# Loading half of b's first slice ahead of a in a fused matmul, GELU, matmul kernel

## Chip, cores and metric

One core of one Trainium2 chip. The metric is the device time of one execution in microseconds (us).

## The reference

```python
def reference(a, b, c):            # a 1024x1024, b 1024x2048, c 2048x1024, all float32
    h = np.matmul(a, b)
    h = 0.5 * h * (1 + np.tanh(np.sqrt(2 / np.pi) * (h + 0.044715 * h ** 3)))
    return np.matmul(h, c)
```

## The kernel before

PE is the engine of the matrix products, DVE and ACT are the vector and the scalar engine, and SP issues the loads. The kernel loads the first four row blocks of a (a0 to a3, 512 KB each) and then the left halves of b's eight row blocks ("slices" b0 to b7, 128 rows of 4 KB, 512 KB each) through one queue. Each block of a is cast to bf16 (DVE one half, ACT the other), transposed on PE and copied into `aT`. Products of zeros, at the start and between the transposes, keep PE busy so that its clock rises; those between are called fillers below. The first real products (k=0) need all four blocks of a and b0; those of k=1 need b1, and so on. What follows k=7 (the rest of the two matrix products) is not touched by the change.

```python
    def load_b0(k, parts):
        st = b0stage.tile([128, W0], F32, name="b0_st")
        w = W0 // parts                                   # W0 = 1024 columns
        for i in range(parts):
            nc.sync.dma_start(out=st[:, ts(i, w)], in_=bv[:, k, ts(i, w)])
        b_st[k] = st

    for mt in R:                                          # a0 .. a3
        load_a0(mt, 1)
    for k in range(KT):                                   # b0 .. b7
        load_b0(k, 1)
    # ... cut
    warm_up(8)                                            # 8 products of zeros
    # ... cut: cast_a0, turn0 (transposes), copy0, cast_b0
    for mt in range(3):
        cast_a0(mt, 0)
        cast_a0(mt, 1)
        pt = [turn0(mt, 0), turn0(mt, 1)]
        if mt == 2:
            cast_a0(3, 0)
        copy0(mt, 0, pt[0])
        copy0(mt, 1, pt[1])
        warm_up((3, 6, 2)[mt])
    copy0(3, 0, turn0(3, 0))                              # with b0's casts inside
    warm_up(2)
    # ... cut
    for t in R:
        mm0(t, (0,))                                      # first k=0 products
    copy0(3, 1, turn0(3, 1))
    for t in (4, 7, 6, 5):
        mm0(t, (0,))
```

Of the kernel before, what the change touches and what calls it, by code (L numbers as in the profile page):

```python
# [9 lines left out]
F32 = mybir.dt.float32  # L10
# [9 lines left out]
def kernel(ctx, tc, a, b, c, out):  # L20
    nc = tc.nc
# [3 lines left out]
    KT = K // 128  # L25
# [4 lines left out]
    W0 = N // 2  # L30
# [5 lines left out]
    bv = b.rearrange("(kt p) n -> p kt n", p=128)  # L36
# [7 lines left out]
    b0stage = ctx.enter_context(tc.tile_pool(name="b0stage", bufs=6))  # L44
# [19 lines left out]
    a_st, b_st = {}, {}  # L64

    def load_a0(mt, parts):
        st = astage.tile([128, K], F32, name="a_st")
        w = K // parts
        for i in range(parts):
            nc.sync.dma_start(out=st[:, ts(i, w)], in_=av[:, mt, ts(i, w)])  # L70
        a_st[mt] = st

    def load_b0(k, parts):
        st = b0stage.tile([128, W0], F32, name="b0_st")
        w = W0 // parts
        for i in range(parts):
            nc.sync.dma_start(out=st[:, ts(i, w)], in_=bv[:, k, ts(i, w)])  # L77
        b_st[k] = st

    gate = consts.tile([128, 1], F32, name="gate")  # L80
    for mt in R:
        load_a0(mt, 1)
    for k in range(KT):
        load_b0(k, 1)

    nc.gpsimd.tensor_copy(gate, b_st[4][:, 0:1])
    g = consts.tile([128, 1], F32, name="g")
# [5 lines left out]
    def warm_up(n):  # L93
        for _ in range(n):
            nc.tensor.matmul(ps[3], warm[:, 0:128], warm, start=True, stop=True)  # L95
# [4 lines left out]
    def cast_a0(mt, g):  # L100
        if g == 0:
            ab.append(abf.tile([128, K], BF16, name="ab1"))
            nc.vector.tensor_copy(ab[mt][:, 0:512], a_st[mt][:, 0:512])
        else:
            nc.scalar.activation(ab[mt][:, 512:K], a_st[mt][:, 512:K], AF.Copy)

    def turn0(mt, g):
        if mt == 2:
            pt = side[g]
        elif (mt, g) == (3, 1):  # L110
            pt = ps[5][:, :].bitcast(BF16).rearrange("p (k m) -> p k m", k=8)
        else:
            pt = tpool.tile([128, 8, 128], BF16, name="pt", tag="pt")
        for k in range(4):
            nc.tensor.transpose(pt[:, k, :], ab[mt][:, ts(4 * g + k, 128)], ident)
        return pt

    def copy0(mt, g, pt):
        dst = aT[0][:, ts(g, 4), ts(mt, 128)]
        if g == 0 and mt == 3:  # L120
            nc.vector.tensor_copy(dst[:, 0, :], pt[:, 0, :])
            cast_b0(0, (0,))
            nc.vector.tensor_copy(dst[:, 1:4, :], pt[:, 1:4, :])
            cast_b0(0, (1,))
        elif g == 0 or mt == 3:
            nc.vector.tensor_copy(dst, pt[:, 0:4, :])
        else:
            nc.scalar.activation(dst, pt[:, 0:4, :], AF.Copy)

    HW = W0 // 2  # L130

    def cast_b0(k, parts=(0, 1)):
        v = {0: ((128, 384), (768, W0)), 1: ((0, 128), (128, HW))}.get(k, ((0, HW),))
        a = {0: ((0, 128), (384, 768))}.get(k, ((HW, W0),))
        for i in parts:
            if i < len(a):
                nc.scalar.activation(b_lo[:, k, slice(*a[i])], b_st[k][:, slice(*a[i])], AF.Copy)  # L137
            if i < len(v):
                nc.vector.tensor_copy(b_lo[:, k, slice(*v[i])], b_st[k][:, slice(*v[i])])  # L139

    for mt in range(3):
        cast_a0(mt, 0)
        cast_a0(mt, 1)
# [6 lines that stand above are left out]
    copy0(3, 0, turn0(3, 0))  # L150
    warm_up(2)
    ps += [ppool.tile([128, H], F32, name="ps", tag="ps") for _ in range(2)]
# [12 lines left out]
    for t in (4, 7, 6, 5):  # L165
        mm0(t, (0,))
    cast_b0(1)
    for k in range(1, KT):
        if k + 1 < KT:
# [15 lines left out]
    for j in R:  # L185
        st = abf.tile([128, K], BF16, name="ab1")
# [288 lines left out]
```

## Time and profile before

| kernel before | |
|---|---|
| device time, median of 6 runs | 120.81 us (120.11 to 121.13) |
| span of the profile | 119.0 us |
| PE busy | 96% |
| a0 lands, a3 lands | about 4.0, about 8.8 us |
| first product of k=0, of k=1 | 10.43, 12.73 us |

The prediction shows most lines of this profile. Five more are needed to compare with later: DVE's first cast of a0 and PE's six fillers from the timeline (start, length, then the instruction; in brackets the idle time before it and what ended it), the DMA view of a0's issue (its last number is the time from issue to landing), and two stretches of the windows view. In the timeline, a line has start, length, then the instruction; in brackets the idle time before it and what ended it. In the windows view, the fields after the stretch are its length, the busy time of PE, PEld, DVE, ACT and POOL, each with its count, then the granted clock, the DMA share and GB/s.

```profile
4.01 0.43 DVE L103 CAST ab<-a_st 128x512 bf16<-128x512 f32 x1 [2.88 <-DMA a_st<-in_a_dram]
...
7.41 1.46 PE L95 MATMUL ps<-warm 128*128 128x512 bf16 x6
...
a_st<-in_a_dram SPq DMA_DIRECT2D x1, 512.0 KB, 3.2
...
2.00:4.00 2.00, 2.00 (x6) 0.76 (x5) 0.00 (x0) 0.22 (x2) 0.00 (x0) 1.00 0.97 369
9.00:11.00 2.00, 1.97 (x17) 1.01 (x15) 1.44 (x6) 1.53 (x4) 0.00 (x0) 1.00 0.87 242
```

Loads run at 369 GB/s while a0 comes in and at 242 GB/s in a slow stretch from 9 to 11 us, where b0 ends and b1 begins. The six fillers take 0.24 us each (1.46 / 6), so the array is at full clock by 7.4 us.

### The profile page before, as it was taken

How to read it: one execution, taken by the hardware profiler on the slowest of the kernel's cores; microseconds unless marked ns; L12 is line 12 of the kernel's file. 1: busy time of each engine (PE TensorE's matmuls, PEld its weight loads, DVE VectorE, ACT ScalarE, POOL GpSimd, SP SyncE). 2: the span in 40 equal slices, each digit the busy share in tenths (PEclk: the TensorE clock that was granted, in tenths of full speed). 3: DMA queues.
4: the chain of work that ended last, by engine and by line, in shares of the span. 5: the costliest groups of instructions: out<-in, count | busy, mean ns of one | idle time of the engine just before them, and what ended most of it. 6: DMA issues, size and time to landing. Idle time of an engine off the chain costs nothing.

```text
span 119.0 us, 1605 instructions
## 1 busy us (share of the span) xinstructions
PE 114.7 (96%) x589; PEld 76.6 (64%) x589; DVE 82.4 (69%) x115; ACT 45.7 (38%) x77; POOL 26.6 (22%) x39
## 2 busy tenths in 40 slices
PE   5999999999999999999999999999999999999990
PEld 2555344479744445888888447888888888886460
DVE  0335433057999927999999999995789992724450
ACT  4366455788423474406269999421000000000000
POOL 2000049752310000086305229100006500000000
PEclk9999999999999999999999999999999999999999
DMA  3999999999999999959999999999997999944434
GB/s 135 379 376 286 419 419 225 169 331 391 232 211 202 206 207 358 361 130 241 258 233 205 191 194 200 182 204 147 149 162 164 248 267 348 348 168 161 175 118 148
DMA packets 13543, 28.41 MB, mean 239 GB/s; under 512 B 992, under 2 KB 5472, under 8 KB 13536
## 3 DMA queue, kind: packets, MB, share of 16 engines
q0 software_dynamic: 9216, 17.83, 72.9%
q1 hardware_dynamic: 4176, 10.42, 23.4%
q8 instruction: 4, 0.07, 0.2%
q10 hardware_dynamic: 144, 0.07, 0.2%
q14 instruction: 3, 0.02, 0.1%
HBM read 20.97 MB, written 4.19 MB: 211 GB/s over the span
## 4 chain that ended last, share of the span: by engine, by line
PE 87%; DMA 8%; SPq 2%; DVE 0%; issue 0%
PE ps L273 63%; PE ps L157 8%; DMA b_st<-in_b_dram 8%; PE ps L211 7%; PE ps L204 4%; PE pt L157 3%; PE ps L197 2%; SPq L70 1%; SPq L77 0%; DVE ot L444 0%; DVE b_lo L139 0%
## 5 line engine op out<-in xcount | busy, mean ns | idle before, releaser
L273 PE MATMUL ps<-t,s 128*128 128x512 f32 x64 | 14.9, 392 | 0.0
L273 PE MATMUL ps<-c,h 128*128 128x512 bf16 (+2 forms) x80 | 14.2, 337 | 0.0
L273 PEld LDWEIGHTS ps<-t,s 128*128 128x128 f32 x64 | 12.0, 188 | 2.6
L281 DVE TENSOR_TENSOR ot<-ps,v 128x512 f32<-128x512 f32 x16 | 10.4, 680 | 3.2 <-PE ps L273 3.2
L273 PE MATMUL ps<-t,h 128*128 128x512 f32 x48 | 11.7, 389 | 0.0
L157 PE MATMUL ps<-aT,b_lo 128*128 128x512 bf16 x48 | 11.6, 380 | 0.1
L175 ACT ACTIVATE h<-ot 128x512 bf16<-128x512 f32 (+1 forms) x16 | 9.4, 623 | 5.9 <-DVE ot L281 5.9
L273 PEld LDWEIGHTS <-h 128*128 128x128 bf16 x80 | 7.1, 98 | 7.0 <-issue 0.5
L175 ACT ACTIVATE h<-ps 128x512 bf16<-128x512 f32 (+2 forms) x17 | 8.3, 526 | 8.4 <-PE ps L211 5.9
L389 DVE TENSOR_TENSOR ot<-ps,p 128x512 f32<-128x512 f32 x11 | 7.5, 687 | 5.3 <-PE ps L273 3.1
L157 PEld LDWEIGHTS <-b_lo 128*128 128x128 bf16 x64 | 6.0, 98 | 7.8 <-DVE b_lo L139 1.0
L273 PEld LDWEIGHTS ps<-t,h 128*128 128x128 f32 x48 | 9.0, 188 | 1.9
L95 PE MATMUL ps<-warm 128*128 128x512 bf16 x21 | 7.7, 511 | 1.2 <-DVE warm L50 1.2
L211 PE MATMUL ps<-aT,b_lo 128*128 128x512 bf16 x40 | 8.8, 379 | 0.0
L291 POOL DMA_DIRECT2D c<-in_c_dram x8 | 6.3, 833 | 6.2 <-DMA b<-in_b_dram 3.9
L273 PE MATMUL ps<-as,bt 128*128 128x512 f32 x32 | 7.6, 396 | 0.0
L273 PE MATMUL ps<-as,b 128*128 128x512 f32 x32 | 7.4, 389 | 0.0
L273 PE MATMUL ps<-c,s 128*128 128x512 f32 x32 | 7.4, 389 | 0.0
L139 DVE CAST b_lo<-b_st 128x512 bf16<-128x512 f32 (+3 forms) x10 | 3.6, 371 | 5.2 <-DMA b_st<-in_b_dram 5.2
L137 ACT ACTIVATE b_lo<-b_st 128x512 bf16<-128x512 f32 (+2 forms) x9 | 5.1, 581 | 5.1 <-DMA b_st<-in_b_dram 5.0
L273 PE MATMUL ps<-aT,bx 128*128 128x512 bf16 x32 | 7.1, 379 | 0.0
L422 POOL DMA_DIRECT2D t<-c x4 | 3.5, 1042 | 15.4 <-PE ps L273 14.3
(73 smaller groups left out, 172.9 us busy)
## 6 DMA issues: line engine op xcount, KB each, us to landing
b_st<-in_b_dram SPq DMA_DIRECT2D x8, 512.0 KB, 9.6
out_dram<-ot SPq DMA_DIRECT2D x15, 256.0 KB, 2.1
c<-in_c_dram POOLq DMA_DIRECT2D x6, 512.0 KB, 17.5
t<-c POOLq DMA_DIRECT2D x6, 512.0 KB, 6.5
a_st<-in_a_dram SPq DMA_DIRECT2D x4, 512.0 KB, 4.9
b<-in_b_dram POOLq DMA_DIRECT2D x2, 1024.0 KB, 11.0
c<-in_c_dram POOLq DMA_DIRECT2D x2, 1024.0 KB, 20.3
t<-t POOLq DMA_DIRECT2D x4, 512.0 KB, 8.6
```

The lines of the kernel that those rows point to most:

```text
L95: nc.tensor.matmul(ps[3], warm[:, 0:128], warm, start=True, stop=True)
L137: nc.scalar.activation(b_lo[:, k, slice(*a[i])], b_st[k][:, slice(*a[i])], AF.Copy)
L139: nc.vector.tensor_copy(b_lo[:, k, slice(*v[i])], b_st[k][:, slice(*v[i])])
L157: nc.tensor.matmul(ps[t], b_lo[:, k, ts(t, 128)], aT[0][:, k, :], start=(k == 0), stop=(k == KT - 1))
L175: nc.scalar.activation(dst, src, AF.Gelu_apprx_tanh)
L204: nc.tensor.matmul(p, b_lo[:, k, ts(t, 128)], aT[1][:, k, ts(q, 256)], start=(k == 0), stop=(k == KT - 1))
L211: nc.tensor.matmul(p, b_lo[:, k, ts(t, 128)], aT[h][:, k, :], start=(k == 0), stop=(k == KT - 1))
L273: nc.tensor.matmul(p, lhs(t)[:, ts(j, 128)], rhs(t)[:, q], start=(t == 0), stop=(t == n - 1))
L281: tt(ot, p, u, op=ADD)
L291: nc.gpsimd.dma_start(out=dst[:, t:t + 4, :], in_=cv[:, r * NH + t:r * NH + t + 4, ts(q, H)])
L389: tt(ot, p, u, op=ADD)
L422: nc.gpsimd.dma_start(out=t2[i], in_=c21[:, P2[i], :], accum_op=ADD)
```

## The change

The intent is to have half of b0 cast while ACT has nothing to do, so that the first products need not wait for b0 and its casts. The first 512 columns of b0 are loaded ahead of a0, the other 512 behind a3; `load_b0` now takes the columns to load.

```diff
+    HW = W0 // 2
+    load_b0(0, slice(0, HW))
     for mt in R:
         load_a0(mt, 1)
-    for k in range(KT):
-        load_b0(k, 1)
+    load_b0(0, slice(HW, W0))
+    for k in range(1, KT):
+        load_b0(k)
 ... in copy0, between the copies of a3's first half:
             nc.vector.tensor_copy(dst[:, 0, :], pt[:, 0, :])
-            cast_b0(0, (0,))
+            cast_b0(0, (1,))
             nc.vector.tensor_copy(dst[:, 1:4, :], pt[:, 1:4, :])
-            cast_b0(0, (1,))
 ... in cast_b0, the columns of k=0:
-        v = {0: ((128, 384), (768, W0)), ...   # DVE
-        a = {0: ((0, 128), (384, 768))} ...    # ACT
+        v = {0: ((0, 0), (768, W0)), ...
+        a = {0: ((0, HW), (HW, 768))} ...
 ... ahead of the loop over a's blocks:
+    cast_b0(0, (0,))
```

More of the change, by code (lines that the diff above doesn't have):

```diff
@@ L71, in load_a0, with load_b0 @@
         a_st[mt] = st
-    def load_b0(k, parts):
-        st = b0stage.tile([128, W0], F32, name="b0_st")
-        w = W0 // parts
-        for i in range(parts):
-            nc.sync.dma_start(out=st[:, ts(i, w)], in_=bv[:, k, ts(i, w)])
-        b_st[k] = st
+    def load_b0(k, c=slice(0, W0)):
+        if k not in b_st:
+            b_st[k] = b0stage.tile([128, W0], F32, name="b0_st")
+        nc.sync.dma_start(out=b_st[k][:, c], in_=bv[:, k, c])
+    HW = W0 // 2
     gate = consts.tile([128, 1], F32, name="gate")
+    load_b0(0, slice(0, HW))
     for mt in R:
         load_a0(mt, 1)
-    for k in range(KT):
-        load_b0(k, 1)
+    load_b0(0, slice(HW, W0))
+    for k in range(1, KT):
+        load_b0(k)
     nc.gpsimd.tensor_copy(gate, b_st[4][:, 0:1])
@@ L128, in copy0 @@
             nc.scalar.activation(dst, pt[:, 0:4, :], AF.Copy)
-    HW = W0 // 2
     def cast_b0(k, parts=(0, 1)):
-        v = {0: ((128, 384), (768, W0)), 1: ((0, 128), (128, HW))}.get(k, ((0, HW),))
-        a = {0: ((0, 128), (384, 768))}.get(k, ((HW, W0),))
+        v = {0: ((0, 0), (768, W0)), 1: ((0, 128), (128, HW))}.get(k, ((0, HW),))
+        a = {0: ((0, HW), (HW, 768))}.get(k, ((HW, W0),))
         for i in parts:
@@ L137, in cast_b0 @@
                 nc.scalar.activation(b_lo[:, k, slice(*a[i])], b_st[k][:, slice(*a[i])], AF.Copy)
-            if i < len(v):
+            if i < len(v) and v[i][1]:
                 nc.vector.tensor_copy(b_lo[:, k, slice(*v[i])], b_st[k][:, slice(*v[i])])
+    cast_b0(0, (0,))
     for mt in range(3):
```

## The prediction

> **What bounds the kernel now.** I began with the page's busy shares: PE is busy for 96% of a 119.0 us span at full granted clock, so only PE's idle time and its start can be won. Next came the chain of work that ended last, by line and then in order of time. The kernel before, page and chain in order of time:
>
> ```profile
> PE 87%; DMA 8%; SPq 2%; DVE 0%; issue 0%
> ...
> 3.20 9.22 DMA b_st<-in_b_dram
> 12.43 0.02 issue
> 12.45 0.24 DVE b_lo L139
> 12.69 0.05 issue
> 12.73 1.52 PE ps L157 x6
> 14.26 0.21 PE pt L157
> ```
>
> The columns of the lines with a number first are start, length, what. From 12.73 us to the end the chain is almost nothing but PE. What starts that run is the landing of b's second slice (k=1) at 12.43, cast by DVE for 0.24. The DMA issued at 3.20 is the sixth of the queue: a0 to a3, b0, b1, 512 KB each. Everything earlier (a's casts and transposes, the k=0 products) matters only if it ends after that landing. Would it? The timeline of the first 16 us, PE and its weight loads, answers:
>
> ```profile
> 9.58 0.39 PE L115 MATMUL pt<-ident,ab 128*128 128x128 bf16 x4
> 9.80 0.59 PE L95 MATMUL ps<-warm 128*128 128x512 bf16 x2
> 10.43 1.04 PE L157 MATMUL ps<-aT,b_lo 128*128 128x512 bf16 x4
> 11.37 0.40 PE L115 MATMUL ps<-ident,ab 128*128 128x128 bf16 x4
> 11.60 0.38 PE L157 MATMUL ps<-aT,b_lo 128*128 128x512 bf16 x1
> 11.81 0.59 PE L157 MATMUL pt<-aT,b_lo 128*128 128x512 bf16 x2
> 12.28 1.98 PE L157 MATMUL ps<-aT,b_lo 128*128 128x512 bf16 x7
> ...
> 10.43 0.55 PEld L157 LDWEIGHTS <-b_lo 128*128 128x128 bf16 x4 [0.53 <-ACT b_lo L137]
> ...
> 12.73 0.10 PEld L157 LDWEIGHTS <-b_lo 128*128 128x128 bf16 x1 [0.60 <-DVE b_lo L139]
> 13.00 0.98 PEld L157 LDWEIGHTS <-b_lo 128*128 128x128 bf16 x6 [0.17 <-DVE b_lo L139]
> ```
>
> The eight k=0 products start at 10.43, behind an ACT cast of b0. The eighth starts at 12.28; at one product each 0.216 us (later 24 take 5.18 in the chain) PE could go on at about 12.50. It waits for b1 until 12.73, so the k=0 work has only about **0.23 us** of slack. The change plays inside that slack.
>
> The same timeline for ACT and DVE shows what the k=0 start waits for:
>
> ```profile
> 8.78 0.43 DVE L103 CAST ab<-a_st 128x512 bf16<-128x512 f32 x1 [0.64 <-DMA a_st<-in_a_dram]
> ...
> 10.00 0.23 DVE L121 COPY aT<-pt 128x128 bf16<-128x128 bf16 x1 [0.45 <-PE pt L115]
> ...
> 9.35 0.60 ACT L128 ACTIVATE aT<-ps 128x512 bf16<-128x512 bf16 x1 [0.63 <-PE ps L115]
> 10.07 0.72 ACT L137 ACTIVATE b_lo<-b_st 128x128 bf16<-128x128 f32 x2
> ```
>
> There are two branches: a3 lands by 8.78 and its first transposed piece is in aT at 10.23 (10.00 + 0.23). On the other side b0 lands at about 10.0 (the DMA view of its issue: 2.59 plus 7.5) and its first cast is done at about 10.38 (10.07 plus 0.31, the least of that ACT group). They are level within 0.15 us.
>
> **What the Trainium skill says.** "DMA: Bandwidth & Descriptors", section "Two DMAs through the same engine are not ordered": within one queue of one engine descriptors start in order. So half of b0 put first delays all of a by its own transfer. The trace agrees: landings of the six loads come in order of issue (a 3.2 to 6.6 us after issue, b0 7.5, b1 9.2). "Perfetto Trace Analysis", section "DMA Optimizations", warns of overhead in transfers below 2 KB; the new halves have rows of exactly 2 KB. From the packet records before: 2 KB packets of the output stores take 84 ns, 4 KB ones of the loads 159 ns, so I count only 2 x 84 - 159 = 9 ns a row. "ScalarE: Activation LUTs", section "What ACT_TABLE_LOAD costs", gives 186 ns + 0.833 N for an ACTIVATE with immediate scale and bias: 612 ns at N=512 and 293 at 128. The trace has 630 and 309, so it agrees, and N=256 should be about 0.41 us (estimate). "TensorE: Matmul & The Clock Gate", section "What's actually happening", says that the array runs at half clock until it has been busy for a window of some 3.4 us. The trace shows warm-up products 0.43 us apart until about 5 and 0.22 later, so a longer hole before the first transposes could matter.
>
> **The change part by part.**
> 1. One load of 512 KB becomes two of 256 KB: one ahead of a, one behind it. The bytes ahead of b1 stay 3 MB (4 x 0.5 + 0.5 + 0.5, b1 included). Eight rows a DMA engine (128 / 16), in two halves, add 8 x 9 ns = 0.07 us. The extra issue on SP costs 0.4 us (row L70, median 0.43), but SP is well ahead: b1 is issued at 3.20 and lands at 12.43. So **b1 lands at about 12.50, +0.07**.
> 2. a moves back by half a slice: 8 rows x 84 ns = **0.67 us** for a0 to a3. a0 4.0 to 4.7, a3 8.75 to about 9.4.
> 3. ACT casts b0's first 512 columns early, alone (0.63), probably at about 3.2 to 3.9, in the 1.78 us in which it now waits for a0. This is free. ACT's two casts at 10.07 (0.72) become one of 256 columns (0.41), and DVE loses one cast of 256 (0.28): neither bounds PE here.
> 4. The first product now needs only a3. Worked forward: a3's cast 9.43 to 9.86; transposes about 10.0, last one out at 10.39 (0.39 for four); DVE copy of the first piece to 10.65; first product **about 10.70 against 10.43, +0.27**, not +0.67, because 0.15 of waiting for the b0 cast and some 0.25 of PE's own queue (cast done 9.21, transposes 9.58) are given back.
> 5. Then four products (0.86) to 11.56, four transposes to 11.79, three products to 12.43, and a3's second half must be copied before the last of them: the DVE copy is then about 11.99 to 12.41, so the last product starts at about 12.43 and PE is free at **12.65**. The small stall at 11.31 (PE waited for ACT's cast of a3) goes, since ACT is done at about 11.13.
> 6. b1's cast is ready at 12.50 + 0.02 + 0.24 + 0.05 = 12.81. That is later than 12.65, so b1's landing still rules, with 0.15 instead of 0.23 of slack.
>
> The sum is 12.81 - 12.73 = **+0.08 us**, with all of the rest PE work that is unchanged. The first product's wait disappears from the path, but it was not on the path.
>
> **The rivals.**
> *The a branch takes over as the bound.* If a moves by more than 0.67, or if ACT and PE casts in the chain a0 to a3 line up badly, the k=0 work ends after 12.81 and each tenth counts in full. For it: slack is only 0.15. Against it: DVE idles 0.64 just before a3's cast, so the earlier slices have room. Worth +0.1 to +0.5 us, or 121.1 to 121.5.
> *The slow stretch of the DMA moves.* The windows view before:
>
> ```profile
> 4.00:8.00 4.00, 4.00 (x24) 2.38 (x23) 1.80 (x5) 2.14 (x4) 0.00 (x0) 1.00 1.02 390
> ...
> 9.00:10.00 1.00, 1.00 (x13) 0.66 (x11) 0.55 (x2) 0.60 (x1) 0.00 (x0) 1.00 0.90 233
> 10.00:11.00 1.00, 0.97 (x5) 0.34 (x4) 0.89 (x4) 0.93 (x3) 0.00 (x0) 1.00 0.85 250
> ...
> 12.00:16.00 4.00, 3.92 (x18) 1.57 (x17) 1.57 (x5) 1.89 (x3) 0.00 (x0) 1.00 1.03 422
> ```
>
> The last column is GB/s. From 9 to 11 us, over the end of b0 and the start of b1, the loads run at 233 to 250 rather than 390 to 422, which costs about 0.8 us (2 us at 241 is 482 KB, or 1.2 us at 406). That is why b1 lands 2.4 after b0, while later slices are 1.28 apart. The trace does not tell why. If half of b read early shifts or ends it, b1 could land up to 0.8 earlier; then the k=0 work rules, and the gain stops at 12.65 - 12.73, about 0.1 us. If it hits a instead, a3 is late and the loss may be 0.5.
> *A cold array.* The warm-up ends at about 4.78, a0's cast then ends near 5.1: PE has a hole of 0.4 us that it has not now. If the clock rises one window later, transposes and warm-up products stretch; perhaps +0.3, and only if it lasts past 9 us.
>
> **Range and chances.** The three times before are 120.11, 121.12 and 121.13: a spread of 1.0 that is far larger than the effect. Their mean is 120.8; with +0.1 to +0.2 (the +0.08 and a little for the rivals on the losing side) I predict **121.0 us**. The range 120.1 to 121.7 takes in that spread and +0.5. Two per cent is 2.4 us, more than everything before the first product could gain by a reordering, so within 2% has 0.98, faster 0.01, slower 0.01.
>
> **What would show each step.** In the profile after: a0's casts at about 4.7 and a3's at about 9.4 (step 2); one ACT cast of b0 before 4.7 (3); first product at about 10.7, its wait now named after DVE's copy (4); last k=0 product at about 12.4 (5); k=1 starting at about 12.8, still behind b1 (6); from there PE unbroken, as long as before. The prediction is wrong if k=1 starts outside 12.5 to 13.3, or if PE has new gaps after it.

## The result, and the profile after

The changed kernel takes **124.38 us** (median of 6 runs, 123.46 to 124.67) against 120.81 us. The ratio is 1.0284, with a 95% interval of 1.0230 to 1.0338: slower by about 2.8%, or 3.6 us between the medians. A ratio here is the mean time of one kernel's fast runs over that of the other's of the same rounds, so it is not quite the ratio of the medians. The profiled run was one of 124.67, with a span of 122.9 us.

The page's chain by engine, and the chain in order of time, of the kernel after (start, length, what; lines left out):

```profile
PE 91%; DMA 5%; DVE 1%; SPq 0%; issue 0%
...
1.18 5.89 DMA a_st<-in_a_dram
...
7.58 1.03 PE pt L116 x8
8.62 1.28 PE ps L96 x3
...
10.75 2.56 PE ps L96 x6
...
16.67 1.54 PE ps L156 x7
```

The chain no longer runs through b1. It runs through the landing of a0 at 7.07 us, then through one cast of DVE (0.44), and from 7.58 through PE alone, fillers (L96) included. The line at 16.67 is the one that stood at 12.73 before: a shift of 3.94 us, as large as the growth of the span (122.9 - 119.0 = 3.9). So all of the loss is made before 16.67, and nothing behind it changed.

The timeline, the DMA view of the first issue, and the same two stretches of the windows view, of the kernel after:

```profile
5.74 0.63 ACT L135 ACTIVATE b_lo<-b_st 128x512 bf16<-128x512 f32 x1 [3.50 <-DMA b_st<-in_b_dram]
7.10 0.43 DVE L104 CAST ab<-a_st 128x512 bf16<-128x512 f32 x1 [5.96 <-DMA a_st<-in_a_dram]
7.58 1.03 PE L116 MATMUL pt<-ident,ab 128*128 128x128 bf16 x8 [2.79 <-DVE ab L104]
10.54 2.77 PE L96 MATMUL ps<-warm 128*128 128x512 bf16 x6
...
b_st<-in_b_dram SPq DMA_DIRECT2D x1, 256.0 KB, 5.0
...
2.00:4.00 2.00, 2.00 (x6) 0.76 (x5) 0.00 (x0) 0.22 (x2) 0.00 (x0) 1.00 0.52 160
9.00:11.00 2.00, 2.00 (x13) 1.19 (x11) 0.64 (x2) 0.98 (x3) 0.00 (x0) 1.00 1.05 406
```

Three things are to be seen. First, the half of b0, 256 KB, needs 5.0 us from issue to landing, longer than the 3.2 us of twice as many bytes of a0 before; from 2 to 4 us the queue moves 160 GB/s with its DMA engines busy for only half of the time. Second, PE is idle for 2.79 us, from 4.79 to 7.58, and then its six fillers take 2.77 us instead of 1.46: the array is at half clock until about 13 us. Third, the slow stretch from 9 to 11 us is gone (406 GB/s). Loads are slow ahead of a instead; whether the same cost has moved there is a question for the experiments.

The clock column deserves a warning. It says 1.00 in every stretch above, also where the fillers take twice their time. The trace has a clock record only from the first change of the clock on, at 13.3 us here. Before that, the durations must be read.

### The profile page after: what moved, and what is told of

Its sections match the earlier page's. It is cut to its first block, busy times and chain, and to the rows that moved or that the text cites.

```text
span 122.9 us, 1605 instructions
## 1 busy us (share of the span) xinstructions
PE 115.9 (94%) x589; PEld 77.2 (63%) x589; DVE 81.9 (67%) x114; ACT 45.5 (37%) x77; POOL 26.2 (21%) x39
## 4 chain that ended last, share of the span: by engine, by line
PE 91%; DMA 5%; DVE 1%; SPq 0%; issue 0%
PE ps L272 61%; PE ps L156 8%; PE ps L210 7%; DMA a_st<-in_a_dram 5%; PE ps L203 4%; PE ps L96 4%; PE pt L156 3%; PE pt L116 2%; PE ps L196 1%; PE ps L116 1%; DVE ab L104 0%; SPq L76 0%; DVE ot L443 0%
## 5 line engine op out<-in xcount | busy, mean ns | idle before, releaser
L96 PE MATMUL ps<-warm 128*128 128x512 bf16 x21 | 9.0, 584 | 1.2 <-DVE warm L50 1.2
L135 ACT ACTIVATE b_lo<-b_st 128x512 bf16<-128x512 f32 (+1 forms) x9 | 5.1, 600 | 7.5 <-DMA b_st<-in_b_dram 7.5
L197 DVE COPY aT<-ps 128x1024 bf16<-128x1024 bf16 x4 | 2.7, 689 | 6.7 <-PE ps L196 6.7
L272 PEld LDWEIGHTS ps<-as,bt 128*128 128x128 f32 x32 | 6.0, 188 | 1.4
```

The source lines that it names most:

```text
L96: nc.tensor.matmul(ps[3], warm[:, 0:128], warm, start=True, stop=True)
L135: nc.scalar.activation(b_lo[:, k, slice(*a[i])], b_st[k][:, slice(*a[i])], AF.Copy)
L197: nc.vector.tensor_copy(aT[1][:, :, ts(j, 128)], pt)
L272: nc.tensor.matmul(p, lhs(t)[:, ts(j, 128)], rhs(t)[:, q], start=(t == 0), stop=(t == n - 1))
```

## The experiments

Twelve kernels were run. "Before" was timed anew beside each group of four: 120.78, 120.83 and 120.84 us in the medians. All results were correct.

**Is it the order of the loads or the casts?** Both halves of b0 behind a, casts split as in the changed kernel:

```diff
-    load_b0(0, slice(0, HW))
     for mt in R:
         load_a0(mt, 1)
+    load_b0(0, slice(0, HW))
     load_b0(0, slice(HW, W0))
 ... and cast_b0(0, (0,)) goes back into copy0
```

> b0 stays in two halves and the casts are split as in the changed kernel, but both halves are loaded behind a. Both theories: the order of loads is all of the loss, so a0 lands at 4.0, the PE has no hole and the time is that of the kernel before, 120.4 to 121.3. If it is over 122, the halving or the casts cost by themselves.

Measured: 121.40 us (120.70 to 122.40, 4 runs), ratio 1.0052 (0.9992 to 1.0111), 0.1 us above the range expected. a0 landed at 4.04, PE had no early hole. The halving and the casts are not the loss of 3.6 us; whether they cost 0.6 is not decided by these runs. In the profile (a run of 121.79) the chain runs through the landing of b0's second half, at 11.73 us, where the whole of b0 had landed at 10.04 before.

**Late a, or cold array?** The changed kernel with more products of zeros at the start:

```diff
-    warm_up(8)
+    warm_up(20)
```

> The changed kernel with 20 in place of 8 products of zeros at the start, enough to reach about 7.6 us. Theory 'late a plus cold array': a0 still lands at about 7.1, but the array is at full clock when the transposes come, the 11 later filler products take 0.22 instead of 0.43 us, and 1.0 to 2.0 of the 3.5 us come back: 122.4 to 123.4. If the late landing alone is the loss, the time stays at 124.0 to 124.7.

Measured: 122.89 us (122.53 to 123.43, 4 runs), ratio 1.0172. The chain in order of time and the timeline of this run:

```profile
1.20 6.99 PE ps L96 x20
...
14.85 1.54 PE ps L156 x7
...
10.08 1.46 PE L96 MATMUL ps<-warm 128*128 128x512 bf16 x6
```

a0 lands as late as in the changed kernel (its casts start at 7.07), but the fillers are back at 1.46 us, and k=1 starts at 14.85. So the shift of 3.94 us in the profiles has two parts: 16.67 - 14.85 = 1.82 for the cold array, and 14.85 - 12.73 = 2.12 for the late a. In the medians, 124.38 - 122.89 = 1.49 come back by warming alone. The split is not exact: the chain of this run begins with the 20 zeros and not with a0, since they last until 8.19, while the changed kernel's transposes began at 7.58. With fewer zeros k=1 might start up to 0.6 us earlier, an estimate from these two figures, and the late a would have that much less. a3 lands at about 10.9 in both runs (before: 8.8) and is in the chain of neither.

**The hole alone, with a on time.** The kernel before with a short warm-up:

```diff
-    warm_up(8)
+    warm_up(2)
```

> The kernel before with 2 in place of 8 products of zeros at the start: loads unchanged, a0 at 4.0, but a hole in PE's work from 2.0 to 4.5. Theory 'the hole costs a cold array by itself': filler products and transposes stay at 0.43 and 0.11 us for at least 3 us longer than before, k=1 starts at 14 to 15 instead of 12.7, and the time is 121.8 to 123.2. If only a late a matters, the time stays at 120.8 plus or minus 0.5.

Measured: 121.08 us (120.34 to 121.81, 20 runs), ratio 1.0026 (1.0006 to 1.0046). This missed the expectation. The profiled run was the slowest of the 20, and there the mechanism is as expected, with k=1 a little earlier than said: fillers cold (six in 2.77 us, at 7.55), k=1 at 13.76, which is 1.03 later than before. But most runs lose little; the mean loss is 0.3 us. So an idle PE at the start makes a late clock possible, it seems, and not certain. The clock records fit this. PE begins at 1.19 or 1.20 us in every profile, yet the first rise of the clock stands at 3.86 us in one (b at a distance of 4 KB, below), at 6.30 with 20 zeros and at 7.22 in the kernel before. The time of the rise in one profile is thus one draw of several, and the 1.49 us of the medians above are a safer figure than the 1.82 of two profiles.

**Is the very first load slow, or loads of b?** b0's half between a0 and a1:

```diff
-    load_b0(0, slice(0, HW))
-    for mt in R:
+    load_a0(0, 1)
+    load_b0(0, slice(0, HW))
+    for mt in range(1, 4):
         load_a0(mt, 1)
 ... and its ACT cast moves behind the casts of a0
```

> The changed kernel with b0's first half between a0 and a1 instead of first; its ACT cast moves behind the first casts of a. Theory 'b first': a0 lands at 4.0 and the array stays warm, but the half costs 1.5 to 3 us there, a1 lands at 6.8 to 8 and a3 at 10 to 11, and the time is 122.2 to 123.2, that of the long warm-up. Theory 'the very first load is slow': the half costs 0.67, a1 lands at 5.9 and a3 at 9.4, and the time is 120.8 to 121.5.

Measured: 122.64 us, two runs of 121.9 and two of 123.5; ratio 1.0166. a0 landed at 4.15, the half at 6.84, 2.7 us later, and a1 at 8.15. The windows view of this run while the half comes in:

```profile
4.00:6.00 2.00, 2.00 (x12) 1.07 (x11) 0.85 (x2) 0.90 (x2) 0.00 (x0) 1.00 0.69 139
```

The slowness goes with the half of b0, not with the place at the head of the queue.

**Narrow rows, or b?** Two runs: all of b0 ahead of a, so with rows of 4 KB; and a0 in two halves of 2 KB rows, b behind a.

```diff
 all of b0 first:
-    load_b0(0, slice(0, HW))
+    load_b0(0)
 ...
-    load_b0(0, slice(HW, W0))

 a0 in halves (from the kernel before):
-        load_a0(mt, 1)
+        load_a0(mt, 2 if mt == 0 else 1)
```

> All of b's first slice (512 KB, rows of 4 KB) goes ahead of a; casts as in the changed kernel. Theory 'narrow rows' (the first load is slow because its rows are 2 KB): b0 lands as a0 did in the kernel before, at about 4.0 us, a0 1.28 later at about 5.3, and the time is 121.5 to 123. Theory 'b first' (whatever of b is read first, cold, is slow, like the stretch from 9 to 11 us before): b0 lands at 6 or later, a0 after 7, and the time is 124.5 or more.

> The kernel before with a0 loaded in two halves of 256 KB with rows of 2 KB; b stays behind a. Theory 'narrow rows': a0's first half lands at about 5 to 5.7 and its second (ACT's cast) at about 7 instead of 4.0, with the PE hole, and the time is 123 to 124.5. Theory 'b first': the first half lands at about 3.0, the second by 4.3, and the time is that of the kernel before, 120.8 plus or minus 0.5.

Measured: all of b0 first, 123.37 us (123.16 to 124.22, 4 runs), ratio 1.0221; a0 in halves, 121.52 us (121.29 to 121.97, 4 runs), ratio 1.0059. The DMA view of the first issue in each, and the windows view of the run with all of b0 first:

```profile
b_st<-in_b_dram SPq DMA_DIRECT2D x1, 512.0 KB, 4.5
...
9.00:11.00 2.00, 1.99 (x8) 1.01 (x9) 1.18 (x3) 1.11 (x2) 0.00 (x0) 0.50 1.02 395
```

```profile
a_st<-in_a_dram SPq DMA_DIRECT2D x1, 256.0 KB, 2.7
```

Rows of 2 KB are not slow: a0's first half lands in 2.7 us. b0 with rows of 4 KB is slower than a0 of the same size (4.5 against 3.2), so neither theory had it whole; the times of both runs lie between the two ranges expected. The a0 run lost 0.7 us because a1 came late, at 7.29 (its chain begins there), behind another slow stretch from 3 to 6 us; why it had that one is open. The windows line also shows the cold array once openly: here the clock had risen at 5.19 and fallen again at 8.60, so the record says 0.50.

**The same bytes of b as whole rows.** 64 rows of 4 KB first, the other 64 behind a, casts late:

```diff
+    nc.sync.dma_start(out=b_st[0][0:64, :], in_=bv[0:64, 0, 0:W0])
     for mt in R:
         load_a0(mt, 1)
+    nc.sync.dma_start(out=b_st[0][64:128, :], in_=bv[64:128, 0, 0:W0])
```

> The same 256 KB of b's first slice ahead of a, but as 64 full rows of 4 KB instead of 128 half rows of 2 KB; the other 64 rows behind a; casts as in the run of the casts alone. Theory 'b first': it is as slow as in the changed kernel, a0 at 6 to 7.1, and the time is 123.3 to 124.8. Theory 'half rows': a0 lands at 4.7 to 5.2, and the time is 121 to 122.3.

Measured: 122.85 us (122.01 to 123.00, 4 runs), ratio 1.0166. The first load took 3.7 us to land and a0 came at 5.47, between the two expectations. From 9 to 11 us, where the other 64 rows and the first of b1 are read, the loads ran at 211 GB/s: the slow stretch came twice, once for each set of rows.

**The tensor, or the distance between the pieces?** Up to here, the slow first loads had been of b, whose rows lie 8 KB apart in memory, and the fast ones of a, whose rows lie 4 KB apart. (Later loads of a could be slow too, as a1 in the run of a0's halves.) Three runs cross the two. Each is the kernel before with one more load of 256 KB at the head of the queue, into a tile that nobody reads:

```diff
+    junk = consts.tile([128, 512], F32, name="junk")
+    # b, pieces 4 KB apart:  b.rearrange("k (h n) -> (k h) n", h=2)[0:128, 0:512]
+    # a, pieces 8 KB apart:  a.rearrange("(r h) k -> r h k", h=2)[0:128, 0, 0:512]
+    # c, pieces 4 KB apart:  c[0:128, 0:512]
+    nc.sync.dma_start(out=junk, in_=<one of the three>)
     for mt in R:
         load_a0(mt, 1)
```

> The kernel before with a 256 KB load that nobody uses put first: 128 pieces of 2 KB of b, each 4 KB after the one before (half of the first 64 rows). Theory 'the pitch' (2 KB pieces 8 KB apart are slow when read first): it lands at 3.0 to 3.6 as a0's half did in the run of a0's halves, a0 lands at 4.5 to 5. Theory 'b itself': it lands at 5 to 6 and a0 at 6.5 to 7.1, as in the changed kernel.

> The same, with 128 pieces of 2 KB of a, each 8 KB after the one before (half of every second row of a). Theory 'the pitch': it lands at 5 to 6 and a0 at 6.5 to 7.1. Theory 'b itself': it lands at 3.0 to 3.6 and a0 at 4.5 to 5. If both this and the run of b at 4 KB land at about 4.4, both factors count, each about half.

> The same, with 128 pieces of 2 KB of c, each 4 KB after the one before; c is a third tensor, not read until 23 us. Theory 'the pitch': it lands at 3.0 to 3.6, a0 at 4.5 to 5. Theory 'any tensor but a is slow first': it lands at 5 or later.

Measured, from the DMA view of the first issue of each run (b at 4 KB, a at 8 KB, c at 4 KB), and the windows view of a at 8 KB:

```profile
junk<-in_b_dram SPq DMA_DIRECT2D x1, 256.0 KB, 2.7
```

```profile
junk<-in_a_dram SPq DMA_DIRECT2D x1, 256.0 KB, 5.0
...
9.00:11.00 2.00, 2.00 (x12) 1.20 (x11) 0.63 (x3) 0.98 (x3) 0.00 (x0) 1.00 1.03 403
```

```profile
junk<-in_c_dram SPq DMA_DIRECT2D x1, 256.0 KB, 2.6
```

| first load: 128 pieces of 2 KB | distance 4 KB | distance 8 KB |
|---|---|---|
| of a | 2.7 us | 5.0 us |
| of b | 2.7 us | 5.0 us (changed kernel) |
| of c | 2.6 us | not run |

The distance decides between these runs and the tensor does not. Pieces 8 KB apart also spread over twice as much memory, 1 MB against 512 KB, and no run varies that alone. Against it speaks that the run of 64 rows read the same 512 KB of b as b at 4 KB here and needed 3.7 us against 2.7; but it also wrote to 64 partitions instead of 128. The run with a at 8 KB takes 124.26 us (two runs), as much as the changed kernel, with b's order and casts left alone. It also lost the slow stretch from 9 to 11 us (403 GB/s, though b is first read there), while b and c at 4 KB kept it (272 and 299 GB/s). Those two runs take 121.76 us (17 fast runs; the one slow run took 123.44) and 122.28 us (2 runs); they pay for 256 KB more.

So most of these runs fit a cost tied to the first loads with pieces 8 KB apart, paid once near the start of the program; put ahead of a it is on the path, behind a most of it is not. That the stretch from 9 to 11 us and the slow first load are one cost is inferred from the one going where the other comes. What makes it is open. The trace shows where it sits: of the 16 DMA engines that share the first load of the changed kernel, seven had landed their share by 3.13 us, the last only at 5.71, while with b at 4 KB all had by 3.44. Two runs limit the rule: in the run of the casts alone the first half of b0, behind a, went at the full pace (0.65 us behind a3) and the stretch came in the second half; with 64 rows at a time it came twice.

**Paying it in small, early.** The kernel before plus a load of b0's first 128 columns (64 KB) that nobody reads, issued by ACT, either at the start or, in the program, after ACT's first ACTIVATE:

```diff
+    touch = consts.tile([128, 128], F32, name="touch")
+    nc.scalar.dma_start(out=touch, in_=bv[:, 0, 0:128])
     for mt in R:                 # early; the late one stands behind the first ACTIVATE
         load_a0(mt, 1)
```

> The kernel before, plus one small load (64 KB: the first 128 columns of b's first slice, into a tile that nobody reads) issued by ACT at the start, beside a0. Theory 'b first, once': the slow stretch at about 9 to 11 us goes, b1 lands at 11 to 11.7 instead of 12.4, a0 is late by no more than 1 us, and the time is 120.3 to 121.2 (the k=0 work then bounds). Theory 'the place in the queue or the time is slow, not the first reading of b': the stretch stays, b1 lands at 12.4 or later.

> The kernel before with the small load of b's first 128 columns issued by ACT after its first ACTIVATE (about 2.2 us) instead of at the start, so that it runs beside a1 and not a0. Expected if an early read of b is what helps: a0 back at 4.0, b1 at 11.9 or earlier as with the early small load, and a time of 120.0 to 120.5. If the late one delays a1 as much as the early one delayed a0, the time is that of the early one or worse, 120.3 to 121.

Measured: early, **120.31 us** (120.16 to 121.25, 20 runs), ratio 0.9970 (0.9951 to 0.9988); late, 120.90 us (20 runs), ratio 1.0023. The windows view of the early one, and its chain:

```profile
9.00:11.00 2.00, 2.00 (x20) 1.16 (x19) 1.18 (x6) 1.39 (x4) 0.00 (x0) 1.00 1.02 299
...
0.74 3.94 DMA a_st<-in_a_dram
...
12.44 1.54 PE ps L159 x7
```

The stretch shrinks (299 instead of 242 GB/s), b1 lands at 11.88 instead of 12.43, and k=1 starts at 12.44, 0.29 earlier. a0 is 0.7 late, and that is now what bounds: the chain begins with a0's landing at 4.68 and not with b1. The late one was not as late as planned: ACT issued it at 1.18 us and not at about 2.2. Its packets ran from 3.4 to 5.3 us, beside a1; a0 was on time, a1 was delayed to 6.74 and k=1 started at 12.93, 0.2 later than before. The early one beats the kernel before, by 0.3% only. That the smaller stretch is the cause is read from one profile, not shown by a run that varies it alone.

## Why the prediction was wrong

- **What bounds the kernel** was read rightly: the time is set by when k=1 can start, and from there PE ran unbroken. The growth of the span equals the shift of that start (3.9 and 3.94 us).
- **Step 1**, b1 at 12.50: it landed at about 12.84, 0.34 later than said. This did not matter, since b1 bounds nothing any more.
- **Step 2 is the step that failed**: "a moves back by half a slice: 8 rows x 84 ns = 0.67 us". That a would be late by the half's own transfer was right; its size was not. a0 moved by 3.1 us, from 4.0 to 7.1, and a3 by 2.1, from 8.8 to 10.9. The 84 ns are right for packets that follow one another (stores, in the middle of the program). They say nothing about a first load with pieces 8 KB apart, where the engines stood idle half of the time. The mis-sized term is that one transfer: 0.67 us assumed, 5.0 us from issue to landing measured, where the same bytes 4 KB apart needed 2.7 and moved a0 by 1.1 (to 5.09).
- **Step 3** was right in kind: ACT's early cast of b0 came before a0 and cost nothing, only at 5.74 instead of 3.2.
- **Steps 4 to 6** fell with step 2: first product at 14.78 (said: 10.70), k=1 at 16.67 (said: 12.81), bound by PE and not by b1. Step 4 also had the path wrong. It let the first product wait for a3 alone, and step 5 had PE free 3.2 us after a3's cast began (9.43 to 12.65). With a warm array, in the long warm-up, k=1 came 3.93 us after a3 (10.92 to 14.85), and a3 was not in the chain: the zeros at the start, then ACT's work on a0 and a1 and PE's own queue were.
- **The rival of the slow stretch** named what happened ("If it hits a instead, a3 is late and the loss may be 0.5"): the right mechanism as far as it is known, sized at a quarter of the 2.1 us by which a3 was late.
- **The rival of the cold array** also came true, sized at "+0.3" where warming gave back 1.5 us. The prediction put the hole at 0.4 us because it took a0 to be at 4.7; with a0 at 7.1 it was 2.8. It also misread the kernel before, where the page's granted clock of 1.00 hides it: the fillers do not go at 0.22 us from about 5 us on. Three of them still need 1.49 us at 5.43, and the first fast ones are the six at 7.41.
- **The chances**: 0.98 for within 2% rested on the sentence that two per cent are "more than everything before the first product could gain". That is a bound on a gain. A loss had no such bound, and it was a loss.

## What to carry to other kernels

Where a slow stretch of the loads is hidden behind other work, moving such a load forward can put it onto the path, so size a load that goes first from a first load of the same layout, and not from packets in the middle of a stream. A late first operand costs twice when it also leaves PE idle: here at most 2.1 us for the wait and 1.5 to 1.8 us for the clock, and of these the second is bought back by more products of zeros. The last landing before a product need not be what it waits for: look in the chain whether it is there. When a profile shows a slow stretch that it doesn't explain, its loss belongs in the range on both sides.

## What the Trainium skill lacked or had wrong

- "DMA: Bandwidth & Descriptors", section "Latency and other measured facts", tells of low rates for row pitches of 2 MiB and more (at 512 KiB the rate is still near the full one), and of no dependence on how many tiles are touched. Here loads with a pitch of 8 KB were slow, and only near the start of a program: 128 pieces of 2 KB took 5.0 us to land at 8 KB and 2.6 to 2.7 us at 4 KB, for two tensors at 8 KB and three at 4 KB; later loads at the same pitch of 8 KB run at 422 GB/s. No page has this.
- "TensorE: Matmul & The Clock Gate", section "What's actually happening", had nothing wrong. A rise some 3.4 us after the start of the work is not what it promises: it calls the window of that length free-running, so that the moment of the rise depends on where in it the work begins. The clock records agree: in the run with all of b0 first the clock stays up for 3.41 us and down for 3.41, and from PE's start at 1.19 us to the first rise it took 2.67 us with b at 4 KB and 6.03 in the kernel before.
- "Perfetto Trace Analysis", section "DMA Optimizations", advises larger transfers against overhead below 2 KB and says nothing of the distance between the pieces. The size was not what counted here: 128 pieces of 2 KB took 2.6 to 2.7 us at 4 KB distance, and rows of 4 KB at 8 KB distance were slow (4.5 us against 3.2 us for 512 KB).
- No page says that the granted clock reads as 1.00 before the first clock record: it did so up to 13.3 us in the changed kernel, while six fillers took 2.77 us in place of 1.46.
